# Hybrid attention and mLSTM block: mLSTM values copied into the mLSTM's load tiles, and the feed-forward shift, scale and gate sums paused over part of the second superblock

## The chip, the cores and the metric

The kernel runs on one core of a Trainium2 chip. The metric is the device time of one execution in microseconds; shown are the median and the spread of three runs, and one further execution that was profiled. A core has five engines with queues of their own: TensorE (PE; PEld is its weight load), VectorE (DVE), ScalarE (ACT), GpSimd (POOL) and SyncE (SP). SP computes nothing here and issues most of the DMA transfers, in order; POOL and ACT issue some.

## The reference

One decoder block over a sequence of 2048 rows of width 1024, in float32:

```
mod = c @ w_ada + b_ada
shift_m, scale_m, gate_m, shift_f, scale_f, gate_f = split(mod, 6)
h = rms_norm(x, g_pre_mix) * (1 + scale_m) + shift_m
q_a, k_a, v_a, q_m, k_m, v_m, o_m, i_m, f_m, g_a, g_m = split(h @ w_in)
y_a = sliding_window_attention(rope(q_a), rope(k_a), v_a, sinks)
q_m, k_m = split(silu(causal_conv4(q_m, k_m)))
y_m = sigmoid(o_m) * head_layer_norm(mlstm(q_m, k_m, v_m, i_m, f_m))
merged = sigmoid(g_a) * (y_a @ w_branch_attn) + sigmoid(g_m) * (y_m @ w_branch_mlstm)
x = x + gate_m * rms_norm(merged @ w_out, g_post_mix)
h2 = rms_norm(x, g_pre_ffn) * (1 + scale_f) + shift_f
x = x + gate_f * rms_norm((silu(h2 @ w_ffn_gate) * (h2 @ w_ffn_up)) @ w_ffn_down, g_post_ffn)
```

Attention has 8 query heads and 2 key heads of 64 with a window of 128 rows; the mLSTM has 4 heads of 128. The feed-forward width is 2816. Of `mod`, the last three parts are the feed-forward's; nothing before the feed-forward reads them.

## The kernel before, in words

The sequence is cut into four blocks of 512 rows, two to a superblock; the text calls them block one to block four (`b` 0 to 3 in the code). Every matrix product is made of three products of rounded parts (`mm3`). The mixer of a superblock runs in this order: attention queries, keys and values ("kv") and the mLSTM values (`vm`) of its first block; kv, queries and mLSTM values of its second block; then fourteen products for both blocks at once (the output gate "om", the mLSTM queries and keys "qk", the branch gates "ga" and "gm"); then the branch outputs of either block. In the first superblock the attention queries and keys of block one come in a start that is written out by hand. The feed-forward follows.

The main products go to four PSUM banks called acc, all others to four called mix. The products of the four groups of 128 rows of a block take one acc bank each, so the next stage can begin only when the copies out of PSUM have freed them. For the mLSTM values that copy is on ACT, line 870, into a tile from the pool tx, from where SP writes it to DRAM (`vm_d`); the mLSTM reads it back chunk by chunk.

The pool tx has nine tiles of 128x512 and serves nearly everything in the mixer: rotated queries and keys until POOL has written them to DRAM (`at_d`), convolutions, gates, rows of x, and the loads of the ada sums. The pool ld has four tiles of the same size. It holds the keys and values of block one, and the mLSTM's chunks of queries and keys; between the two it is free. The pool tm has nine tiles.

The `mod` sums are made on DVE: `ada_stream` loads eight pieces of `w_ada` for each half of a part (line 476, 256 KB each, on SP), and adds each, times its piece of c, into an accumulator in tm (lines 465 and 467). It is one of several Python generators that run beside the main stream of products: each says after how many ns of an estimated PE time it wants its next turn, and `tick` gives the turns between products. The stream for the feed-forward's three parts starts in the branch outputs of block one with a gap of 9000 and must be through by the branch outputs of block four (`finish(R_ada)`).

Beside it run `hprep`, which makes the normalised rows of the second block, `hsums`, which splits sums of both blocks for the fourteen products (DMA line 569, casts line 575), the attention (`attention`: tile of inputs loaded at line 954, scores copied at line 985, masked at line 987) and the mLSTM.

After the hand-written start the instructions' order on each engine is set by a scheduler from priorities and a timeline of its own; it also gives out the pools' tiles. So a change of a tile's pool or of a generator's turns can move other instructions.

Of the kernel before, what the change touches and what calls it, by code (L numbers as in the profile page):

```python
# [19 lines left out]
P = 128  # L20
# [53 lines left out]
def decoder_block(ctx: ExitStack, tc: tile.TileContext, a: dict, out: bass.AP, dbg=None):  # L74
# [386 lines left out]
    def ada_terms(acc, raw, k0, kn):  # L461
        for k in range(kn):
# [3 lines left out]
            else:  # L466
                V.scalar_tensor_tensor(acc, raw[:, k, :], c_, acc, op0=ALU.mult, op1=ALU.add)

    def ada_stream(parts, gap):
        for part, kind in parts:  # L470
            for ch in range(2):
                c0 = part * D + ch * 512
                acc = tm([P, 512])
                for k in range(KD):
                    raw = tx([P, 1, 512])
                    nc.sync.dma_start(raw, w_ada[:, c0:c0 + 512].rearrange("(p k) c -> p k c", k=KD)[:, k:k + 1, :])
                    yield gap
                    ada_terms(acc, raw, k, 1)
                if kind == "gate":
                    br = tx([1, 512])  # L480
                    nc.sync.dma_start(br, a["b_ada"][:, c0:c0 + 512])
                    yield gap
                    V.tensor_tensor(acc[0:1, :], acc[0:1, :], br, op=ALU.add)
                ada_tail(acc, part, ch, kind)
                yield gap
# [283 lines left out]
    def superblock(sb):  # L769
# [96 lines left out]

        def vm(b):
            def evac(t, ps):
                v = tx([P, 512])
                A.copy(v, ps)  # L870
                nc.sync.dma_start(vm_d[b][:, t, :], v)
            if b > 1:
                yield from token_group(kept_weights("vm"), KD, 512, lhs_h(b), evac, kept=True)
            else:
                yield from token_group(srcs_rows(w_in, KD, C_VM), KD, 512, lhs_h(b), evac, store="vm" if b else None)
# [406 lines left out]
        def outputs(b):  # L1282
# [41 lines left out]
            def before_out():  # L1324
                if b == 0:
                    finish(R["ada_m"])
                    R_ada.append(spawn(ada_stream([(4, "scale"), (3, "shift"), (5, "gate")], 9000.0)))
                if b == b1 and b + 1 < NBLK:
                    HC.clear()
                    hps[b + 1] = spawn(hprep(b + 1))  # L1330
                    rope_tables(sb + 1)
                R["gg"] = big([2, D])[:, 0, :]
                nc.sync.dma_start(R["gg"], gg_m_d)
                if b == b0:
                    end_attention(2 * NT)
                    load_y(b1, 0)
                    load_g(b1, 0)
# [15 lines left out]
        if sb == 0:  # L1353
            raws, rotated = {}, {}

            def late_q(t):
                yield from q_stream(b0, t, rope(raws[t], HQ, b0, t))

            def q_raw(t, ps):
                raws[t] = tx([P, 512])  # L1360
                A.copy(raws[t], ps)
                if t > 1:
                    R["qk"].append(spawn(late_q(t), L_KV0 + L_LATE * (t - 1)))

            def q_rope(t):
                rotated[t] = rope(raws[t], HQ, b0, t)

            def q_rest(t):
                for _ in q_stream(b0, t, rotated[t]):
                    pass  # L1370

            first.update(kv=kv0, evac=q_raw, rope=q_rope, rest=q_rest)
        else:
            yield start
            yield from q0
            yield from kv0
            yield lambda: attend(b0)
        yield from vm(b0)
# [8 lines left out]
        yield from vm1[:len(vm1) // 4]  # L1387
        yield lambda: attend(b1)
        yield from vm1[len(vm1) // 4:]

        def start_f():
            finish([hps["t"]])
# [30 lines left out]
    R_ada = []  # L1423
# [831 lines left out]
```

## Time and profile before

| | us |
|---|---|
| median of three runs | 2659.16 (2657.73 to 2660.38) |
| the profiled execution | 2668.66 |
| its span, first to last instruction | 2667.0 |
| PE busy in the span | 2615.5 (98%) |
| DVE busy | 1937.2 (73%) |
| ACT busy | 1281.9 (48%) |
| mean granted clock of PE | 0.994 |

A busy PE is one that has a product under way; it may run at half clock, which the granted clock tells. Everything that the change touches lies between 60 and about 1200 us of the span; the feed-forward begins near 1380 us.

### The profile page before, as it was taken

The numbers are of one execution on the slowest core, as the hardware profiler recorded it, in microseconds if no ns is written. First come the engines' busy times: TensorE is split into PE (matmuls) and PEld (weight loads), VectorE is DVE, ScalarE is ACT, GpSimd is POOL, SyncE is SP. The second block draws the span as 40 slices with busy tenths as digits, with TensorE's granted clock in tenths as the row PEclk, the third lists the DMA queues.
The fourth block names the chain that finished last, engine by engine and source line by source line (L and its number), as shares of the span: only waits on it lengthen the run. The fifth ranks groups of instructions, "written<-read, shape, count | busy, mean of one in ns | idle before, by whom it ended". The sixth has DMA issues, their size and how long they took to land.

```text
span 2667.0 us, 36229 instructions
## 1 busy us (share of the span) xinstructions
PE 2615.5 (98%) x12546; PEld 2145.8 (80%) x12546; DVE 1937.2 (73%) x3758; ACT 1281.9 (48%) x2531; POOL 300.3 (11%) x473
## 2 busy tenths in 40 slices
PE   8999999999989999999999999999999999999998
PEld 6877788888876788888878888888778888888876
DVE  5878887768676988875777777775776767676466
ACT  6656544545654654454643433345554333333444
POOL 0320001101132000210001111110000011001000
PEclk9899999999999999999999999999999999999999
DMA  7785465887787545597765554446675323234556
GB/s 270 255 303 164 135 196 183 291 301 253 262 313 244 166 135 181 183 296 268 220 238 193 184 169 153 163 139 228 213 242 173 111 99 116 90 111 139 199 196 220
DMA packets 327032, 532.97 MB, mean 200 GB/s; under 512 B 23136, under 2 KB 197724, under 8 KB 320064
## 3 DMA queue, kind: packets, MB, share of 16 engines
q1 hardware_dynamic: 287752, 448.45, 50.4%
q0 software_dynamic: 20880, 66.41, 6.6%
q10 hardware_dynamic: 18216, 15.79, 1.9%
q8 instruction: 99, 1.62, 0.2%
q14 instruction: 85, 0.70, 0.1%
HBM read 367.61 MB, written 154.57 MB: 196 GB/s over the span
## 4 chain that ended last, share of the span: by engine, by line
PE 88%; DVE 4%; DMA 3%; ACT 2%; issue 1%; POOL 0%; ACTq 0%; SPq 0%; DVEq 0%; POOLq 0%
PE acc L212 62%; PE mix L212 22%; PE mix L217 2%; PE acc L90 1%; DVE hl L1745 1%; PE mix L90 1%; DMA raw<-as_d 1%; ACT hl L1744 1%; DMA big<-big 0%; DMA raw<-ws_d 0%; DMA raw<-in_w_in_dram 0%; ACT tm L1002 0%; DMA at_d<-tx 0%; DMA raw<-in_w_ffn_down_dram 0%; ACT big L575 0%
## 5 line engine op out<-in xcount | busy, mean ns | idle before, releaser
L212 PE MATMUL acc<-big,hl 128*128 128x512 f32 x3936 | 936.4, 393 | 7.0 <-ACT tx L870 5.4
L212 PEld LDWEIGHTS acc<-big,hl 128*128 128x128 f32 x3936 | 733.8, 188 | 166.4 <-ACT tx L870 5.9
L1744 ACT CAST hl<-raw 128x512 fp32r<-128x512 f32 x732 | 439.9, 621 | 489.6 <-PE acc L212 208.7
L1745 DVE TENSOR_TENSOR hl<-raw,hl 128x512 fp32r<-128x512 f32 x732 | 495.1, 692 | 198.4 <-ACT hl L1744 196.0
L212 PE MATMUL acc<-whi,big 128*128 128x512 f32 (+1 forms) x896 | 281.6, 390 | 3.0 <-ACT tx L870 3.0
L212 PE MATMUL mix<-big,hl 128*128 128x512 f32 x1056 | 263.0, 390 | 1.8 <-ACT hl L1744 1.1
L212 PE MATMUL acc<-hl,hl 128*128 128x512 f32 x1008 | 237.2, 393 | 6.2 <-DVE hl L1745 3.3
L212 PEld LDWEIGHTS mix<-big,hl 128*128 128x128 f32 x1056 | 197.8, 188 | 44.5 <-ACT hl L1744 2.0
L212 PEld LDWEIGHTS acc<-hl,hl 128*128 128x128 f32 x1008 | 187.1, 188 | 51.8 <-DVE hl L1745 8.8
L212 PEld LDWEIGHTS acc<-whi,big 128*128 128x128 f32 x896 | 168.6, 192 | 36.2 <-ACT tx L870 3.4
L212 PE MATMUL mix<-hl,hl 128*128 128x512 f32 x792 | 182.7, 391 | 3.4 <-ACT hl L1744 2.6
L212 PEld LDWEIGHTS mix<-hl,hl 128*128 128x128 f32 x792 | 147.8, 188 | 37.6 <-ACT hl L1744 4.2
L212 PE MATMUL acc<-wlo,big 128*128 128x512 f32 (+1 forms) x448 | 174.4, 389 | 0.0
L212 PE MATMUL acc<-big,whi 128*128 128x512 f32 x512 | 157.3, 393 | 0.0
L268 DVE TENSOR_TENSOR wlo<-raw,whi 128x1024 fp32r<-128x1024 f32 (+1 forms) x76 | 90.8, 1194 | 65.7 <-ACT whi L267 60.2
L267 ACT CAST whi<-raw 128x1024 fp32r<-128x1024 f32 (+1 forms) x76 | 78.4, 1032 | 109.7 <-PE acc L212 103.5
L492 POOL TENSOR_TENSOR rs<-ms,halves 128x1 f32<-128x1 f32 (+1 forms) x56 | 41.3, 744 | 797.8 <-DVE ms L490 750.4
L212 PE MATMUL mix<-hcT4h,hl 128*128 128x512 f32 x352 | 115.6, 389 | 0.7 <-ACT hl L1744 0.7
L212 PE MATMUL acc<-hcT2h,hl 128*128 128x512 f32 x352 | 115.5, 389 | 0.0
L212 PEld LDWEIGHTS acc<-big,whi 128*128 128x128 f32 x512 | 95.3, 188 | 19.3
L212 PEld LDWEIGHTS acc<-wlo,big 128*128 128x128 f32 x448 | 85.8, 192 | 18.0 <-issue 1.2
L212 PE MATMUL acc<-big,wlo 128*128 128x512 f32 x256 | 97.6, 392 | 0.0
(388 smaller groups left out, 3802.3 us busy)
## 6 DMA issues: line engine op xcount, KB each, us to landing
as_d<-w POOLq DMA_DIRECT2D x154, 256.0 KB, 2.5
raw<-in_w_in_dram SPq DMA_DIRECT2D x36, 1024.0 KB, 5.4
raw<-as_d SPq DMA_DIRECT2D x70, 512.0 KB, 3.8
raw<-in_w_ffn_gate_dram SPq DMA_DIRECT2D x22, 1024.0 KB, 6.1
raw<-in_w_ffn_up_dram SPq DMA_DIRECT2D x22, 1024.0 KB, 5.8
raw<-ws_d SPq DMA_DIRECT2D x40, 512.0 KB, 4.6
tx<-in_w_ada_dram SPq DMA_DIRECT2D x64, 256.0 KB, 5.3
g_d<-tx SPq DMA_DIRECT2D x64, 256.0 KB, 2.4
```

The costliest lines, as they stand in the source:

```text
L90: self.last = tc.keep_in_program_order(f(*p, **k)).ins
L212: T.matmul(o, lhsT=lhsT, rhs=rhs, start=start, stop=stop, skip_group_check=resumed)
L217: T.transpose(o, i, ident[:k, :k])
L267: A.copy(hv, src)
L268: V.tensor_tensor(lv, src, hv.bitcast(F32), op=ALU.subtract)
L492: G.tensor_tensor(r[:, :n], ms[:, :n], nhalf[:, :n], op=ALU.pow)
L1744: A.copy(v(hi), src)
L1745: V.tensor_tensor(v(lo), src, v(hi).bitcast(F32), op=ALU.subtract)
```

## The change

Three edits. The mLSTM values of all four blocks are copied into ld tiles instead of tx tiles. A flag pauses `ada_stream` before its next load: it is set ahead of block three's keys and values and cleared after block four's mLSTM values. The stream's gap is 8000 instead of 9000.

```diff
+    held = [False]
+
+    def hold(on):
+        held[0] = on
+
     def ada_stream(parts, gap):
...
                 for k in range(KD):
+                    while held[0]:
+                        yield 1000.0
                     raw = tx([P, 1, 512])
...
             def evac(t, ps):
-                v = tx([P, 512])
+                v = ld([1, 512])[:, 0, :]
                 A.copy(v, ps)
                 nc.sync.dma_start(vm_d[b][:, t, :], v)
...
-                    R_ada.append(spawn(ada_stream([(4, "scale"), (3, "shift"), (5, "gate")], 9000.0)))
+                    R_ada.append(spawn(ada_stream([(4, "scale"), (3, "shift"), (5, "gate")], 8000.0)))
...
             yield from q0
+            yield lambda: hold(True)
             yield from kv0
...
         yield from vm1[len(vm1) // 4:]
+        yield lambda: hold(False)
```

Line numbers above 466 are seven to nine higher in the changed kernel (870 becomes 877, 476 becomes 483). The same instructions are issued in both kernels, but the order differs on every engine from block one's mLSTM values to the end of the mixer; the feed-forward's order is the same from about its first products on. Three places:

ACT in block one, from the first value copy to the attention's scores; acc are the banks of the mLSTM values, `big` the split sums. Before:

```order
L870 COPY tx_1104<-acc_938 128x512
L870 COPY tx_1113<-acc_939 128x512
L267 CAST whi_1134<-raw_935 128x528
L829 CAST tx_912<-mix_989 128x128
L803 ACTIVATE tx_945<-mix_1015 128x512
L803 ACTIVATE tx_950<-mix_1024 128x512
L575 CAST big_1495<-big_1149 128x512 x4
L870 COPY tx_1122<-acc_940 128x512
L870 COPY tx_1131<-acc_941 128x512
L985 COPY tm_1279<-mix_1281 128x256
```

Now:

```order
L877 COPY ld_1104<-acc_938 128x512
L877 COPY ld_1113<-acc_939 128x512
L877 COPY ld_1122<-acc_940 128x512
L267 CAST whi_1134<-raw_935 128x528
L836 CAST tx_912<-mix_989 128x128
L810 ACTIVATE tx_945<-mix_1015 128x512
L810 ACTIVATE tx_950<-mix_1024 128x512
L582 CAST big_1495<-big_1149 128x512 x4
L877 COPY ld_1131<-acc_941 128x512
L992 COPY tm_1279<-mix_1281 128x256
```

The third copy has moved ahead of the weight cast, the rotated keys and queries and the four casts; the fourth still stands behind them. On PE the first half of block two's key products for the third group of rows has moved with it, ahead of the first scores.

SP before block four's keys: `raw<-w_kv_d` is the load of half of the key weights, `big<-big` the copies of the split sums, `at<-at_d` an attention tile. Before:

```order
L476 DMA tx_7553<-in_w_ada_dram 128x512
L476 DMA tx_7713<-in_w_ada_dram 128x512
L569 DMA big_8010<-big_6927 128x2048
L954 DMA at_7481<-at_d_198 128x1792
L569 DMA big_8012<-big_6529 128x2048
L333 DMA raw_7547<-w_kv_d 128x2112
L476 DMA tx_7798<-in_w_ada_dram 128x512
L328 DMA whi_8117<-w_q_d 128x1024
L328 DMA wlo_8118<-w_q_d 128x1024
L333 DMA raw_7721<-w_kv_d 128x2112
```

Now:

```order
L576 DMA big_7999<-big_6930 128x2048
L576 DMA big_8001<-big_6529 128x2048
L333 DMA raw_7548<-w_kv_d 128x2112
L328 DMA whi_8103<-w_q_d 128x1024
L328 DMA wlo_8104<-w_q_d 128x1024
L961 DMA at_7482<-at_d_198 128x1792
L333 DMA raw_7716<-w_kv_d 128x2112
L878 DMA vm_d_212<-ld_7880 128x512
```

The ada loads are gone from here, and the attention tile stands behind the first key load and a query load. On PE half of block four's key products now stand ahead of the first 24 score products instead of behind them. From block three's value weights to the first load of "om", SP has nine ada loads before and none now; DVE has eight ada sums (line 465 or 467) from block three's gate scan to the softmax of its second score tile, and none now.

SP at the first load of the "om" weights (`in_w_in_dram`), at the end of block four's mLSTM values. Before:

```order
L476 DMA tx_8463<-in_w_ada_dram 128x512
L954 DMA at_8488<-at_d_202 128x1792
L1908 DMA raw_8480<-in_w_in_dram 128x8x256
L569 DMA big_8857<-big_6528 128x2048
L954 DMA at_8490<-at_d_203 128x1792
L569 DMA big_8859<-big_6926 128x2048
L1908 DMA raw_8557<-in_w_in_dram 128x8x256
L476 DMA tx_8662<-in_w_ada_dram 128x512
```

Now:

```order
L878 DMA vm_d_213<-ld_8720 128x512
L878 DMA vm_d_213<-ld_8790 128x512
L1917 DMA raw_8447<-in_w_in_dram 128x8x256
L576 DMA big_8818<-big_6528 128x2048
L576 DMA big_8820<-big_6929 128x2048
L1917 DMA raw_8524<-in_w_in_dram 128x8x256
L483 DMA tx_8825<-in_w_ada_dram 128x512
L961 DMA at_8455<-at_d_202 128x1792
```

Both weight loads now stand ahead of the attention tiles and the ada load, and two of the four value writes stand ahead of them. On PE the first 64 "om" products now follow block four's values directly; before, 12 score products stood between. The last ada load has moved from the gates "gm" to just ahead of the mLSTM's last load of values (`vmt<-vm_d`).

## Rows read from the trace of the kernel before

**Rows 1.** The page's part 1, busy time and share of the span.

```profile
PE 2615.5 (98%) x12546; PEld 2145.8 (80%) x12546; DVE 1937.2 (73%) x3758; ACT 1281.9 (48%) x2531; POOL 300.3 (11%) x473
```

**Rows 2.** Waits of PE, 60 to 880 us: total us, times, longest.

```profile
PE acc L212 <- ACT tx L870: 8.4, 4, 4.6
```

**Rows 3.** Timeline of PE: start, length, operation, count [idle before, releaser].

```profile
108.97 0.59 PE L212 MATMUL acc<-whi,big 128*128 128x264 f32 x1 [2.69 <-ACT tx L870]
...
766.18 6.15 PE L212 MATMUL acc<-raw,big 128*128 128x264 f32 x36 [4.18 <-ACT tm L985]
...
774.34 6.13 PE L212 MATMUL acc<-raw,big 128*128 128x264 f32 x48
...
784.73 1.06 PE L217 MATMUL mix<-ident,tm 128*128 128x128 f32 x8 [2.64 <-DVE tm L987]
...
800.75 0.65 PE L212 MATMUL mix<-tm,at 128*64 128x256 f32 x4 [1.26 <-ACT tm L1014]
...
858.72 7.34 PE L212 MATMUL acc<-big,hl 128*128 128x512 f32 x24 [4.55 <-ACT tx L870]
865.99 1.69 PE L212 MATMUL mix<-at 64*128 64x256 f32 x24
...
872.55 17.16 PE L212 MATMUL acc<-big,hl 128*128 128x512 f32 x74
```

**Rows 4.** Timeline of ACT.

```profile
108.34 0.59 ACT L870 COPY tx<-acc 128x512 f32<-128x512 f32 x1 [3.58 <-issue]
...
857.05 1.14 ACT L1744 CAST hl<-raw 128x512 fp32r<-128x512 f32 x2 [8.55 <-DMA raw<-in_w_in_dram]
858.09 1.07 ACT L870 COPY tx<-acc 128x512 f32<-128x512 f32 x2
```

**Rows 5.** Windows: length, busy PE, PEld, DVE, ACT, POOL, granted clock, DMA share, GB/s.

```profile
118.00:121.00 3.00, 3.00 (x16) 3.00 (x14) 0.60 (x3) 2.99 (x13) 0.00 (x0) 0.50 1.04 360
121.00:124.00 3.00, 3.00 (x20) 2.45 (x20) 1.65 (x13) 2.10 (x9) 1.75 (x2) 0.92 0.14 54
...
769.00:770.00 1.00, 1.00 (x7) 1.00 (x6) 1.00 (x4) 0.17 (x1) 0.00 (x0) 0.50 0.95 331
```

**Rows 6.** Timeline of SP, which issues DMA.

```profile
752.22 1.46 SPq L333 DMA_DIRECT2D raw<-w_kv_d  x1
...
845.62 0.40 SPq L1908 DMA_DIRECT2D raw<-in_w_in_dram  x1
...
851.95 9.66 SPq L476 DMA_DIRECT2D tx<-in_w_ada_dram  x2
...
1157.41 0.37 SPq L1084 DMA_DIRECT2D vmt<-vm_d  x1
```

**Rows 7.** DMA, 740 to 775 us; of an issue KB and us to landing.

```profile
DMA packets 2965, 11.42 MB, mean 326 GB/s; under 512 B 498, under 2 KB 498, under 8 KB 2448
...
raw<-w_kv_d SPq DMA_DIRECT2D x2, 1056.0 KB, 14.9
```

**Rows 8.** Timeline of DVE.

```profile
781.54 0.74 DVE L467 SCALAR_TENSOR_TENSOR tm<-tx,c_sb,tm 128x512 f32<-128x512 f32 x1
...
784.15 0.77 DVE L987 COPY_PREDICATED tm<-m_prev,mix 128x256 f32<-128x256 uint32 x2
...
798.04 0.75 DVE L467 SCALAR_TENSOR_TENSOR tm<-tx,c_sb,tm 128x512 f32<-128x512 f32 x1 [3.83 <-DMA tx<-in_w_ada_dram]
798.71 0.68 DVE L1035 TENSOR_TENSOR tm<-mix,tm 128x512 fp32r<-128x512 f32 x1
```

**Rows 9.** Windows after the pause, columns as in rows 5.

```profile
1030.00:1060.00 30.00, 30.00 (x146) 25.10 (x145) 27.73 (x51) 13.14 (x25) 1.66 (x1) 1.00 0.66 213
...
1150.00:1180.00 30.00, 30.00 (x164) 25.44 (x163) 19.51 (x61) 14.44 (x24) 4.11 (x4) 1.00 1.00 319
```

**Rows 10.** Lines 476 and 467: duration ns min/median/max, first and last start.

```profile
L476 SPq DMA_DIRECT2D tx<-in_w_ada_dram x64: 327/429/9170, 294.5 to 1071.1; - x64
...
L467 DVE SCALAR_TENSOR_TENSOR tm<-tx,c_sb,tm x56: 721/744/1543, 300.8 to 1078.2; 128x512 f32<-128x512 f32 x56
```

## Prediction

> **What bounds the kernel now.** I read the engine shares first: TensorE (PE) is busy for 98% of the span [rows 1], so the kernel can become faster only where PE stands still or runs slowly, not by taking work off another engine. The next view is the list of what PE waited for between 60 and 880 us, the stretch that holds everything the change touches before the sums resume. Its largest entry is the copies of the mLSTM values out of PSUM (line 870), 8.4 us in four waits [rows 2]; all its entries together are 18.8 us. The PE timeline shows the places: 2.69 us in block one, 4.18 us before block four's keys, 2.64 and 1.26 us in the attention beside them, 4.55 us before the first product of the output gate, "om" [rows 3]. Between 302 and 766 us and between 859 and 1381 us the timeline has no wait of 0.2 us or more.
>
> A wait costs more than its length here. After the 2.69 us wait the granted clock is 0.50 (1.2 GHz) until about 121.5 us: it is still 0.50 in 118 to 121 and 0.92 in 121 to 124 [rows 5]. It is also 0.50 in 769 to 770, after the 4.18 us wait [rows 5]. Products after it show the price: 36 key products took 6.15 us, 0.171 us each, where 48 took 6.13 us, 0.128 us each, a little later [rows 3]. That is 36 x 0.043 = 1.55 us lost. After the 4.55 us wait 24 products took 7.34 us, 0.306 each, against 74 in 17.16, 0.232 each [rows 3]: 1.8 us lost. After the 2.64 and 1.26 us waits the products run at their usual pace.
>
> **What the waits really end on.** The profile puts a wait down to what came last, so I read the other engines at each place.
> - Block one: ScalarE (ACT) is idle for 3.58 us before the last value copy at 108.34 [rows 4]. PE needs that copy because block two's key products use the same four PSUM banks. What the copy lacks is a tx tile, which is held by slow writes of attention keys to DRAM.
> - Block four to "om": ACT is idle for 8.55 us, and not for a tile: it waits for the gate's weights, issued at 845.62 [rows 6], casts them at 857.05, and only then comes to the copies at 858.09 [rows 4]. The tile alone is not what is late there.
> - Block four's keys: their weights were issued at 752.22 [rows 6] and such a load needs 14.9 us to land in a stretch where DMA moves 326 GB/s [rows 7]. PE goes on at 766.18, as they land.
> - Attention at 784.73: PE waits for VectorE's masked copies (line 987), which start at 784.15 behind two ada sums of 0.74 us, the first at 781.54 [rows 8].
> - Attention at 800.75: VectorE stood 3.83 us at 798.04 for the data of an ada sum; the attention output (line 1035) is behind it at 798.71 [rows 8], and PE's wait follows from that.
>
> **The change, term by term.** Gains are positive. Each has the value I take and its two ends.
>
> Term 1, block one's copies. The first three find an ld tile whose key and value writes were issued early; the fourth waits for the write of the first copy's values. It stands behind the same four casts that the third stood behind before, so it can run about where the third did, well ahead of 108.34. The 2.69 us go, and of the half-clock time (12.5 us from 108.97 to 121.5) what was PE's own: at the 41% that the row at 766.18 shows (1.55 us lost in the 3.8 us until 770) this is 5.1 us. ScalarE is full in a part of it (2.99 of 3 us in 118 to 121 [rows 5]), so I take 4. Sum 6.7; ends 0 (the new tile is as late as the old) and 7.8.
>
> Term 2, the small copy waits of blocks one and two: 8.4 - 2.69 - 4.55 = 1.2 us. From block two on nothing else holds the ld tiles. I take 1.1; ends 0 and 1.2.
>
> Term 3, block four's keys. In SP's order the attention tile (1792 columns, 0.92 MB) moves from ahead of this load to behind it, and no ada load stands beside it. At 326 GB/s [rows 7] 0.92 MB is 2.8 us. Of 4.18 us about 1.4 stay, and the clock does not fall (1.5 us). But the attention tile and the second half of the key weights are later by as much, and PE uses both within 8 us: I charge 2 us. Sum 4.18 - 1.4 + 1.5 - 2 = 2.3; ends -1 and 5.7. A rule bears on this: the Trainium skill, DMA: Bandwidth & Descriptors, section on queues, rings and completion order, says that each DMA engine consumes one ring's descriptors in ring order and takes turns between rings. By it an ada load issued after the key load cannot delay it, and the pause gives nothing here; the move of the attention tile alone would count. By share of bytes instead, the ada loads that leave this stretch would be worth about 3 us. No run here shows which holds.
>
> Term 4, VectorE in the attention. The order has eight ada sums fewer between block three's gate scan and the softmax of its second score tile; two of them (1.48 us) stand just ahead of the masked copies, and one made the 3.83 us stall. I take 1.4 of 2.64 and 1.2 of 1.26: 2.6; ends 0 and 3.9.
>
> Term 5, the "om" weights. Their load moves ahead of the attention tile and of an ada load on SP. With 2.8 us less ahead of it, 4.55 shrinks to about 1.7, and the clock does not fall: 2.8 + 1.8 = 4.6, I take 4.5. PE asks for the products earlier, since 12 scores of about 0.07 us no longer precede them (24 take 1.69 us by the row between); that is why not more. Ends 1 and 6.35. Also gone is the block of SP at 851.95, 9.66 us for two ada loads that wait for tiles [rows 6], from its old place; it reappears one place later, ahead of later weights.
>
> Term 6, what the moved sums cost. Eight more sums fall after the pause, at 0.744 us [rows 10] 6 us of VectorE. It is busy for 27.73 of 30 us in 1030 to 1060 at worst, and 19.51 of 30 in 1150 to 1180 [rows 9], and PE has no wait there: cover enough, cost nothing. Without it they would cost their 6 us. The last ada load moves from 1071.1 [rows 10] to just ahead of the last value load, which ran at 1157.41 [rows 6]: before the sums are needed, so nothing is forced. The sums' accumulator holds a tm tile through the pause, but it held one before, too. New waits from the reordering are unknown; the nearest rows give one of the smallest kind that halved the clock, 2.69 + 1.55 = 4.2 us. I take that; ends 0 and 10.
>
> The sum is 6.7 + 1.1 + 2.3 + 2.6 + 4.5 - 4.2 = 13.0 us; the ends add up to about -10 and +25. It is made against the profiled execution, 2668.66 us with a span of 2667.0, which is 9.5 us above the median of 2659.16. Some of that excess may lie in these crowded stretches, so I take 12 off the median: 2647.
>
> **The rivals.**
> A. The weights stay late. In 8.55 us ACT waited for weights and not for a tile [rows 4], and at 752.22 the key load had no ada load of the last few us ahead of it, so the pause may free nothing for either load. Terms 3 and 5 are then -1 and 1; with 4, 1 and 2 for the others and 3 for new waits the gain is 4 us: 2655. For it: two of the three big waits end on DMA, and the bytes are only moved. Against: the attention tile does move behind both loads. The ring-order rule of the Trainium skill's DMA page (DMA: Bandwidth & Descriptors) points to this case for the pause, and against it for the tile.
> B. Slower. The last ada loads now fall where DMA is full (share 1.00 in 1150 to 1180 [rows 9]), and each that waits for a tx tile holds SP, as at 851.95 for 9.66 us. Two such holds ahead of the branch weights or the attention outputs are 19 us in which the next weights are not issued. PE now has its weights well ahead there; it decides from the point at which the holds exceed this lead by more than the 12 us gained. With all 19 on PE: 2659 - 12 + 19 = 2666. Against: only one load falls there.
> C. Nothing. Block one's fourth copy waits for its new tile as long as before, and elsewhere the copies never bound; gains of 3 to 4 are eaten by the 4.2 of new waits: 2659.
> D. Everything goes, and the clock holds throughout: 25 us, 2634.
>
> **How the numbers follow.** Forecast 0.58, A 0.20, B 0.08, C 0.07, D 0.07. The likeliest case alone spans 2640 to 2653. The range 2638 to 2658 takes in A and leaves out D, B and part of C, about 0.18. A change of 0.2%, 5.3 us, is about what can be told from none. Faster by more: 0.58 + 0.07 + two thirds of A = 0.78. Slower: B and a little of C, 0.09. The rest, 0.13, is the same.
>
> **What would show it.** Right: no PE wait on the value copies in blocks one and two, and a clock of 1.00 from 107 to 121 us; the wait before block four's keys under 2 us; no ada sums on VectorE in 760 to 800; the wait before "om" under 2 us. Wrong: a new PE wait of over 3 us with half clock behind it in 750 to 880, or waits in 1100 to 1220 behind SP's ada loads. If the 4.18 and 4.55 us waits stand as they were, it is A.

## The result, and the profile after

Over 22 runs of each the changed kernel takes 2669.44 us (2662.1 to 2672.93) and the kernel before 2662.04 us (2657.73 to 2665.7). The ratio of the times is 1.0026, with a 95% interval of 1.0021 to 1.0032: slower by about 7 us, where 12 us of gain were forecast. The profiled execution of the changed kernel took 2668.51 us. That of the kernel before, on which the prediction rests, took 2668.66, which is 6.6 us above that kernel's own median of 22 runs; so a second execution of it was profiled (2661.18 us, span 2659.5). It is called the second profile of before, and the comparisons below are made with it where they can be.

PE's busy time is the old one; the changed kernel loses its time elsewhere, not in a larger amount of work:

```profile
PE 2616.6 (98%) x12546; PEld 2143.3 (80%) x12546; DVE 1940.2 (73%) x3758; ACT 1280.7 (48%) x2531; POOL 302.6 (11%) x473
```

PE's timeline after. The line numbers of this part are seven to nine higher than before, as said ahead of the prediction.

```profile
113.27 0.69 PE L217 MATMUL mix<-ident,tm 68*128 68x68 f32 x4 [3.97 <-DVE tm L919]
...
759.39 6.09 PE L212 MATMUL acc<-raw,big 128*128 128x264 f32 x48 [0.78 <-DMA raw<-w_kv_d]
...
777.52 1.17 PE L217 MATMUL mix<-ident,tm 128*128 128x128 f32 x8 [1.44 <-DVE tm L994]
780.26 2.96 PE L212 MATMUL mix<-tm,at 128*64 128x256 f32 x12 [1.57 <-DVE tm L994]
...
849.04 15.67 PE L212 MATMUL acc<-big,hl 128*128 128x512 f32 x64 [1.98 <-ACT hl L1753]
...
926.54 0.98 PE L212 MATMUL mix<-at 64*128 64x256 f32 x12 [1.56 <-DMA at<-at_d]
...
1166.20 4.14 PE L212 MATMUL acc<-big,hl 128*128 128x512 f32 x10 [3.05 <-ACT tx L1242]
1177.26 3.01 PE L212 MATMUL acc<-big,hl 128*128 128x512 f32 x12 [1.80 <-ACT tx L1894]
```

Set beside [rows 3]: the 2.69 us wait of block one is gone, but a wait of 3.97 us for the mLSTM's gate-scan rows stands 4 us later; 4.18 us before block four's keys are now 0.78; 2.64 us in the attention are now 1.44 and 1.57 in two pieces; 4.55 us before "om" are now 1.98. At 1166 and 1177 us stand two waits where the kernel before had none.

To see where the time goes, waits, half clock and slow stretches of PE together, I worked out a lost time: every product counted at the median distance to the next start for its shape at full clock (the same sum for all products in all these kernels), and the sum up to a place taken from the time at which PE reaches it. The program is cut at equal amounts of product work; a column's name is the time of that place in the second profile of before. Lost us of each stretch:

```
              60-  240-  740-  900- 1000- 1140- 1190- 1380-
             240   740   900  1000  1140  1190  1380  2658
before      15.1   2.4  20.1   0.8   0.8   0.6   1.9  20.9
before, 2nd 11.5   1.9  19.7   0.8   0.8   0.6   2.0  18.1
after       12.8   3.0  13.1   4.2   0.8   8.9   2.4  17.3
ld_only     11.8   2.8  25.2   2.5   0.8   0.6   2.0  19.3
ld_early    10.8   2.8  23.0   0.8   0.8   0.7   2.0  18.7
no_pause    12.7   3.0  25.6   3.5   0.8   0.1   2.2  18.7
gap9000     10.5   2.8  18.2  10.1   0.9   0.6   3.0  18.3
no_ld       12.9   2.3  18.8   0.5   0.8  14.8   2.4  19.5
gm_dve      11.2   3.0  13.6   4.2   0.8   6.3   2.6  17.4
tanh_late   12.1   2.9  14.4   4.3   0.8   7.6   2.5  27.5
late_only   12.8   2.2  16.7   1.9   0.8   7.4   2.5  29.9
lockstep    11.3   3.0  16.1   3.8  25.9   1.4   2.0  18.5
no_ld_ls     9.5   2.5  15.5   2.1  29.0   3.1   3.5  23.3
pb8         11.4   3.0   9.9   5.7   0.8   0.5   6.7  18.5
no_ld_pb8    9.7   2.3  16.2   1.0   0.8   0.4   4.9  17.7
cu5000      11.3   4.6  15.2   3.0   0.8   0.2   2.0  18.5
pause_cu    12.6   5.6  15.2   0.9   0.8   0.2   2.0  17.3
pause_cu2   12.6   3.9  14.4   1.8   0.8   0.2   2.0  17.9
p9_4500      9.8   4.7  18.2   7.9   0.4   0.2   2.1  16.7
```

Against the second profile of before, the changed kernel gains 6.6 us in 740 to 900, where the prediction sought its gain, loses 3.4 in 900 to 1000, loses 8.3 in 1140 to 1190, and 1 to 2 in each of the first two. All eight columns together give 7 us more, as the medians do. In the columns up to 1000 the differences depend by 1 to 2 us on how the products are grouped by shape (in coarser groups the gain in 740 to 900 comes out as 7.8 and the loss in 900 to 1000 as 4.6); the loss at 1140 to 1190 does not. The one large loss, then, lies at the branch gates of block four ("gm"), some 300 us behind the pause.

What goes on there is read on three engines of the changed kernel. First SP: the last eight loads of the gate's sum, of which these are the last four (the other four start at 1080.82, 1084.42, 1099.61 and 1101.80):

```profile
1116.88 1.00 SPq L483 DMA_DIRECT2D tx<-in_w_ada_dram  x1
1125.10 0.33 SPq L483 DMA_DIRECT2D tx<-in_w_ada_dram  x1
1131.33 0.33 SPq L483 DMA_DIRECT2D tx<-in_w_ada_dram  x1
...
1164.70 0.75 SPq L483 DMA_DIRECT2D tx<-in_w_ada_dram  x1
```

Then DVE, the sums that read them; line 465 is the first of a half, and the first row here is the last sum of the half before:

```profile
1061.38 0.74 DVE L467 SCALAR_TENSOR_TENSOR tm<-tx,c_sb,tm 128x512 f32<-128x512 f32 x1
...
1174.45 0.48 DVE L465 TENSOR_SCALAR tm<-tx,c_sb 128x512 f32<-128x512 f32 x1
...
1182.80 0.74 DVE L467 SCALAR_TENSOR_TENSOR tm<-tx,c_sb,tm 128x512 f32<-128x512 f32 x1
```

No sum runs between 1061.38 and 1174.45. Seven of the nine tx tiles are loaded by 1131.33 and then only held. In the kernel before each sum follows its load: in the second profile the eight loads run from 1014.58 to 1066.18 and the sums from 1020.58 to 1073.19. Last ACT, which copies the gates out of PSUM into tx tiles (lines 1894, 1900, 1242):

```profile
1142.25 0.58 ACT L1900 COPY tx<-acc 128x512 f32<-128x512 f32 x1 [9.79 <-DMA g_d<-tx]
...
1163.77 1.91 ACT L1264 ACTIVATE big<-big 128x2048 f32<-128x2048 f32 x1
1165.58 0.56 ACT L1242 COPY tx<-acc 128x512 f32<-128x512 f32 x1
...
1174.82 1.91 ACT L1264 ACTIVATE big<-big 128x2048 f32<-128x2048 f32 x1 [1.02 <-DMA big<-g_d]
1176.64 0.57 ACT L1894 COPY tx<-acc 128x512 f32<-128x512 f32 x1
```

A copy at 1142.25 has waited 9.79 us until a tile was free again: it had to be written to DRAM first. Both copies for which PE waits stand directly behind an activation of 1.91 us. So either the tiles or the activations, or the DMA traffic beside both, could be the cause; the experiments took these apart.

### The profile page after: what moved, and what is told of

Read it like the earlier page. It is cut to its first block, busy times and chain, and to the rows that moved or that the text cites. A ratio compares the mean times of both kernels' runs of the same rounds, so it can differ in the third digit from the quotient of the medians.

```text
span 2666.8 us, 36223 instructions
## 1 busy us (share of the span) xinstructions
PE 2616.6 (98%) x12546; PEld 2143.3 (80%) x12546; DVE 1940.2 (73%) x3758; ACT 1280.7 (48%) x2531; POOL 302.6 (11%) x473
## 4 chain that ended last, share of the span: by engine, by line
PE 89%; DVE 5%; DMA 4%; ACT 1%; issue 1%; SPq 0%; POOL 0%; ACTq 0%; DVEq 0%; POOLq 0%
PE acc L212 62%; PE mix L212 23%; PE mix L217 2%; PE acc L90 1%; DVE hl L1754 1%; PE mix L90 1%; ACT hl L1753 1%; DMA raw<-w_kv_d 1%; DMA at<-at_d 0%; DMA raw<-in_w_ffn_down_dram 0%; DMA raw<-ws_d 0%; DMA raw<-as_d 0%; DMA big<-g_d 0%; DMA big<-big 0%; DVE w L2064 0%
```

## The experiments

### The parts of the change alone

A ratio in this section is to 18 to 27 runs of the kernel before, made on the same chip as the experiment's own 4 to 12. Four kernels undo one or two parts each; the pieces of the edits are shown together. `ld_only` has the copies into ld tiles alone; `no_ld` the pause and the gap of 8000; `no_pause` the copies and the gap; `gap9000` the copies and the pause.

```diff
-                v = ld([1, 512])[:, 0, :]
+                v = tx([P, 512])
...
-            yield lambda: hold(True)
...
-                    R_ada.append(spawn(ada_stream([(4, "scale"), (3, "shift"), (5, "gate")], 8000.0)))
+                    R_ada.append(spawn(ada_stream([(4, "scale"), (3, "shift"), (5, "gate")], 9000.0)))
```

> Only the value copies go to ld tiles; no pause, gap 9000. Theory (ACT's order at the branch gates costs the time): ACT has the copies of the last gate products ahead of the branch gates' activations, as before the change, so there is no loss at 1160 to 1180 us; block one keeps its 1.8 us, so about 2660 us where before has 2662, within 0.2%. Rival 1 (late ada loads hold tx tiles and fill DMA at 1100 to 1160): the last ada load lies where it lay before, so also about 2660. Rival 2 (the ld copies themselves cost the time, by the wait for the gate scan in block one): about 2669.

> The change without its first part: copies into tx tiles, pause and gap 8000 kept. Theory: ACT has the same order at the branch gates as in the changed kernel, so waits of about 3.0 and 1.8 us come at 1160 to 1180 us, and the time is 2669 to 2671 us. Rival 1: the same, 2669 to 2671. Rival 2: about 2662 or less.

> The change without its pause: ld copies and gap 8000. Theory: the stream ends before 1071 us and ACT's order at the branch gates is that of before, so no wait over 0.3 us at 1140 to 1200 us; the waits of 2 to 5 us at 760 to 860 us come back; about 2660 us. Rival 1: about 2660 too. Rival 2: about 2669.

> The change with the old gap of 9000: ld copies and pause. The last ada loads fall still later than in the changed kernel, among the last loads of mLSTM values and behind them, but ACT has the copies ahead of most of the branch gates' activations, as before the change. Theory: the pause keeps its 4 to 6 us at 760 to 900 us and nothing is lost at 1160 to 1180 us: 2654 to 2658 us. Rival 1: the loads and their tiles are in the way more than in the changed kernel: 2669 us or more, with PE waits of over 1.5 us at 1140 to 1200 us.

> The kernel before, profiled once more, to see how much its waits differ between executions. No theory is at stake: about 2662 us. If the profile on which the prediction rests overstated the waits at 760 to 870 us, they are some 2 to 5 us shorter here.

Measured: `ld_only` 2666.10 us, ratio 1.0014 (1.0005 to 1.0023); `no_ld` 2675.70, 1.0044 (1.0030 to 1.0058); `no_pause` 2671.10, 1.0029 (1.0018 to 1.0040); `gap9000` 2672.57, 1.0032 (1.0019 to 1.0045). No part alone is faster than before. The table shows three separate costs.

The loss at 1140 to 1190 needs the pause and the gap of 8000 together: 8.9 and 14.8 with both, under 1 with one. In `no_ld` the same two copies are late, by more:

```profile
1168.65 1.66 PE L212 MATMUL acc<-big,hl 128*128 128x512 f32 x6 [3.05 <-ACT tx L1242]
...
1183.25 5.15 PE L212 MATMUL acc<-big,hl 128*128 128x512 f32 x12 [6.91 <-ACT tx L1894]
```

With a gap of 9000 the last half's loads are spread from 1109.50 to 1210.21, and only four are out by 1149.17; PE loses nothing there. But an earlier half is loaded ahead of its sums: seven pieces between 711.91 and 893.21, the first sum at 918.37. PE then waits for a gate's copy, and 10.1 us go in 900 to 1000. From `gap9000`, the first sum on DVE, then the wait on PE:

```profile
918.37 0.48 DVE L465 TENSOR_SCALAR tm<-tx,c_sb 128x512 f32<-128x512 f32 x1
```

```profile
924.54 5.92 PE L212 MATMUL acc<-big,hl 128*128 128x512 f32 x13 [5.93 <-ACT tx L1894]
```

The copies into ld tiles without the pause cost at 740 to 900: 25.2 and 25.6 against 19.7 (of this 3.3 us come in `ld_early`, below, too, whose copies there are those of before). PE comes to the "om" products before their split weights (hl) are ready. From `ld_only`, then `no_pause`:

```profile
862.57 7.77 PE L212 MATMUL acc<-big,hl 128*128 128x512 f32 x22 [2.85 <-DVE hl L1753]
```

```profile
866.24 4.21 PE L212 MATMUL acc<-big,hl 128*128 128x512 f32 x9 [4.03 <-DVE hl L1753]
```

With the pause, in `after`, this stretch costs 13.1 (18.2 in `gap9000`). So there the pause and the copies help each other, and the change does what it says.

The second profile of before also shows how much one execution's waits say. In it PE waited 1.52 and 2.06 us in block one where the first profile has 2.69:

```profile
107.05 0.39 PE L212 MATMUL acc<-whi,big 128*128 128x264 f32 x1 [1.52 <-ACT tx L870]
111.54 0.44 PE L217 MATMUL mix<-ident,tm 68*128 68x68 f32 x4 [2.06 <-DVE tm L912]
...
761.82 6.15 PE L212 MATMUL acc<-raw,big 128*128 128x264 f32 x36 [4.28 <-ACT tm L985]
```

The granted clock was back at 1.00 by 118, where [rows 5] has 0.50 in 118 to 121 (columns as there):

```profile
118.00:121.00 3.00, 3.00 (x23) 2.82 (x24) 2.58 (x14) 2.52 (x9) 1.73 (x2) 1.00 0.52 199
```

From 760 to 870 us it has nearly the waits of the first, 4.28, 2.64, 1.01 and 4.31 against 4.18, 2.64, 1.26 and 4.55, so those were not overstated.

### Late activations or late tiles

My first theory was that the two activations of 1.91 us ahead of the copies on ACT make PE wait. `gm_dve` makes the copies of the last two "gm" products of blocks three and four on DVE instead; `tanh_late` forces the first two activations behind a copy by a bias of zeros that DVE makes out of that copy's tile; `late_only` is `tanh_late` with ld tiles in blocks three and four only.

```diff
-            A.copy(u, v)
+            (V.tensor_copy if by_dve[0] else A.copy)(u, v)
...
```

```diff
+                             bias=late[1] if (b, i) == (2, 0) else 0.0)
...
+            if late[0]:
+                late[1] = small.tile([P, 1], F32, tag="late", name=nm("late"), bufs=1)
+                V.tensor_scalar(late[1], R["U2"][:, 0:1], 0.0, None, op0=ALU.mult)
```

> The changed kernel, with the copies out of PSUM of the last two gate products of blocks three and four on DVE instead of ACT; PE's order is the same up to there. Theory (these copies stand on ACT behind two activations of 1.9 us): the waits of 3.05 and 1.80 us at 1166 and 1177 us are gone or under 0.8 us, the clock stays full there, and the time is about 8 us shorter, 2660 to 2663 us. Rival 1 (the copies lack a tx tile or DMA is full): the waits stay, on whichever engine copies, and the time is about 2669 us.

> The changed kernel, in which the first two activations of block three's branch gates read a column of zeros made from the last gate product's third copy, so that ACT cannot have them ahead of the copies of the gate products before it. The ada loads and PE's order up to there are those of the changed kernel. Theory (the loss at 1150 to 1180 us is those two activations ahead of copies and of the mLSTM's work on ACT): the waits of 3.05 and 1.80 us are under 1 us each, the loss there is 0 to 2 us instead of 9, and the time is 2660 to 2663 us. Rival 1 (the ada loads there, their tiles and their share of DMA): the loss stays near 9 us and the time is 2669 us. In between, as with the copies on DVE (6 us lost): both.

> The run before this one, with ld tiles for the values of blocks three and four alone and tx tiles for blocks one and two. If the copies into ld gain in block one what the prediction said, this is 2 to 7 us slower than the run before it; if the wait there only goes over to the gate scan, it is the same or 1 to 2 us faster: 2659 to 2662 us.

Measured: `gm_dve` 2663.74 us, ratio 1.0009 (1.0000 to 1.0018), yet 6.3 us are still lost at the place; `tanh_late` 2681.94, 1.0077 (1.0065 to 1.0090), with 7.6 lost there; `late_only` 2681.28, 1.0075 (1.0062 to 1.0087), with 7.4. PE's timeline in `gm_dve`, then in `tanh_late`:

```profile
1163.68 0.33 PE L217 MATMUL mix<-ident,tm 128*128 128x128 f32 x1 [1.10 <-ACT tm L1163]
...
1168.41 1.92 PE L212 MATMUL acc<-big,hl 128*128 128x512 f32 x4 [2.28 <-DVE tx L1898]
```

```profile
1168.99 1.20 PE L212 MATMUL acc<-big,hl 128*128 128x512 f32 x4 [1.59 <-ACT tx L1243]
...
1176.25 0.49 PE L212 MATMUL mix<-cst,tm 128*128 128x129 f32 x2 [1.99 <-POOL tm L1108]
```

Whichever engine copies, and wherever the activations stand, the wait only changes its name. That theory fell. In `tanh_late` ACT, with no activation of 1.91 us ahead of it, waits with a copy for the first sum (line 465), which starts at 1176.66 and is the first to read one of the eight pieces:

```profile
1177.17 0.58 ACT L1899 COPY tx<-acc 128x512 f32<-128x512 f32 x1 [1.81 <-DVE tm L465]
```

The 2664 us of `gm_dve` against 2669 are not explained by the 2.6 us gained at the place, and I don't claim them. What `tanh_late` and `late_only` lose in the feed-forward is told at the end.

### Held tiles or the bytes

Two theories were left: the tiles that the eight pieces hold, or the 2 MB that they add to a full DMA. `lockstep` ties each load of the last half to the sum before it, by writing a column of the accumulator into the tile first; `no_ld_ls` is the same with values in tx. `pb8` loads the eight pieces into two tiles of the pool `big`, so that they hold no tx tile, and `no_ld_pb8` does it with values in tx.

```diff
+                    if (part, ch) == (5, 1):
+                        if k == 0:
+                            V.memset(acc[:, 0:1], 0.0)
+                        V.tensor_copy(raw[:, 0, 0:1], acc[:, 0:1])
```

```diff
-                    raw = tx([P, 1, 512])
+                    if (part, ch) == (5, 1) and k < 8:
+                        if k % 4 == 0:
+                            four = big([4, 512])
+                        raw = four[:, k % 4:k % 4 + 1, :]
+                    else:
+                        raw = tx([P, 1, 512])
```

> The changed kernel, in which each load of the last half of the gate's sum waits for the sum before it (a column of the accumulator is copied into the load's tile ahead of the load). In the changed kernel eight such pieces are loaded between 1081 and 1165 us and added only from 1174 us on, so that seven of the nine tx tiles are held from 1131 us. Theory (the held tiles make the gate copies late and cost the 9 us; that ACT has activations ahead of them follows from it): at most two tiles are held, PE has no wait over 1 us at 1140 to 1200 us, and the time is 2659 to 2663 us, although the loads and their bytes now lie wholly in 1140 to 1200 us or behind it. Rival 1 (the loads' share of DMA there): 2669 us or more.

> The same with tx tiles for the values. Without lockstep this version had waits of 3.05 and 6.91 us at 1168 and 1183 us and 2675.7 us. Theory: both waits go, about 14 us, so 2660 to 2663 us; against the run before this one it shows whether the ld tiles gain anything beside the pause. Rival 1: 2675 us.

> The changed kernel, with the eight pieces of the last half of the gate's sum loaded into two tiles of the pool big instead of eight of tx. PE's order is that of the changed kernel up to the gates gm. The eight loads, 2 MB, now stand on SP all at the place of the last one, ahead of block three's last loads, so that their bytes fall at about 1145 to 1170 us, and their sums as late as before. Theory (held tx tiles): the gate copies get tiles in time, PE has no wait over 1 us at 1140 to 1200 us, and the loss there is 0 to 2 us instead of 9: 2659 to 2663 us. Rival 1 (bytes on full DMA): more bytes than in the changed kernel fall there, so 9 us or more are lost and the time is 2669 us or more.

> The same with tx tiles for the values, to which 2675.7 us belong with the pieces in tx. Theory: the waits of 3.05 and 6.91 us at 1168 and 1183 us go, so 2660 to 2663 us; the difference to the run before this one is what the ld tiles are worth beside the pause. Rival 1: 2675 us.

Measured: `lockstep` 2684.97 us, ratio 1.0090 (1.0076 to 1.0104); `no_ld_ls` 2693.19, 1.0119 (1.0103 to 1.0136). They told nothing on the question: the loss at 1140 to 1190 is down to 1.4 and 3.1, but the order moved, and 25.9 and 29.0 us are lost before it, where PE stands for the mLSTM's chain, as in this row of `lockstep`:

```profile
1115.06 0.47 PE L217 MATMUL mix<-ident,tm 128*128 128x128 f32 x1 [3.89 <-DVE tm L1101]
```

`pb8` took 2661.36 us, ratio 0.9999 (0.9990 to 1.0008), and `no_ld_pb8` 2661.78, 1.0000 (0.9991 to 1.0009): 8 us below `after`, and 14 below `no_ld`, with 8.4 and 14.4 us fewer lost at 1140 to 1190. In `pb8` the eight loads leave SP in one burst, some 10 us ahead of the place where PE waited in `after`. SP, DVE and the windows of `pb8`:

```profile
1151.69 4.02 SPq L488 DMA_DIRECT2D big<-in_w_ada_dram  x6
1156.93 0.97 SPq L488 DMA_DIRECT2D big<-in_w_ada_dram  x2
```

```profile
1165.80 0.48 DVE L465 TENSOR_SCALAR tm<-big,c_sb 128x512 f32<-128x512 f32 x1
...
1175.90 0.75 DVE L467 SCALAR_TENSOR_TENSOR tm<-big,c_sb,tm 128x512 f32<-128x512 f32 x1
```

```profile
1160.00:1170.00 10.00, 10.00 (x60) 8.68 (x59) 7.71 (x14) 5.02 (x11) 1.29 (x1) 1.00 1.04 421
```

The same window of `after`:

```profile
1160.00:1170.00 10.00, 6.95 (x30) 5.52 (x29) 4.48 (x21) 8.02 (x13) 2.85 (x3) 0.83 1.06 337
```

More bytes pass in `pb8` (421 GB/s against 337), DMA is as full in both, and PE is busy throughout at full clock where in `after` it stands for three tenths of the window and half of the rest of it is slow. So the bytes are not the cause. Three things differ: no tx tile is held, all loads but the last are some 25 to 70 us later, and ACT's order at the gates is another one. Its first activation of 1.91 us starts at 1160.35 in `after`, and at 1172.99 in `pb8`, behind copies again, as in the kernel before. The scheduler gives out the tiles and sets the order by them, so I take that order as what the held tiles do; changed alone, in `tanh_late`, it left 7.6 us of the loss. A kernel that loads early into tiles of neither pool was not tried. `pb8` loses 4.3 us more than `after` in 1190 to 1380, where PE waits 2.04 us at 1202.50 for a load into a `big` tile, and 3.2 less in 740 to 900, where PE's order is the same; that its whole gain equals the loss taken away is in part luck.

### A smaller gap after the pause; block one

If the pieces are held because the stream comes late to its end, a smaller gap after the pause should bring the last half forward, to where before has it. `cu5000` is the changed kernel with that; `pause_cu` has it with values in tx (`pause_cu2` repeats it); `p9_4500` goes from 9000 to 4500, with values in tx. `cu5000_ms` also zeroes the gate-scan rows early on POOL, for block one's new wait. `ld_early` is the kernel before with ld tiles for blocks one and two only.

```diff
-                    yield gap
+                    yield 5000.0 if resumed[0] else gap
...
```

```diff
-                v = tx([P, 512])
+                v = ld([1, 512])[:, 0, :] if b < 2 else tx([P, 512])
```

> The changed kernel, with a gap of 5000 instead of 8000 once the pause is over, so that the last ada load lies ahead of the gates gm, earlier than before the change. Theory: ACT then has the copies ahead of the branch gates' activations, nothing is lost at 1140 to 1200 us, and 760 to 900 us is as in the changed kernel: 2660 to 2663 us. Rival 3 (the pause costs its time where the sums are resumed, at 860 to 1000 us, by DVE and DMA work): more sums fall there, so waits of some us at 860 to 1000 us and 2669 us or more.

> The kernel of the run before this one, with the zeroing of the gate scan's rows issued on POOL ahead of the gate products of each block instead of within the scan. In the changed kernel DVE waits 1.05 us for this zeroing, behind POOL's writes of attention keys, before PE's 3.97 us wait in block one. If POOL is what bounds block one, the wait at 113 us falls to about 2.9 us and the time by 1 to 2 us. If DVE's own work ahead of the scan bounds it, the wait stays over 3.5 us and the time is the same.

> The pause alone, with the sums made up early: tx tiles for all value copies, gap 8000 up to the pause and 5000 after it. Theory: the pause is worth some 3 to 6 us at 750 to 900 us, and nothing is lost at 1140 to 1200 us, so 2657 to 2661 us. If the pause gains only together with the ld tiles, it is 2662 us or more.

> The pause alone with tx tiles, gap 8000 and 5000, timed once more on the chip of the run before this one: 2657 to 2660 us, 0.1 to 0.2% under the kernel before.

> The pause alone with tx tiles, gap 9000 up to it and 4500 after it. The pause with a gap of 8000 up to it lost 3.7 us at 650 to 700 us, where the old gap loses nothing, and gained the rest. Theory: that loss goes and the gain at 750 to 900 us stays, so 2654 to 2657 us. If the loss at 650 to 700 us comes from the pause and not from the gap, 2658 us.

> The kernel before, with ld tiles for the values of blocks one and two alone; no pause, gap 9000. Theory (in blocks three and four the earlier copies let PE run into split weights of om that are not ready, which cost the run with ld tiles alone its time at 850 to 870 us; in block one nothing is gained): 2661 to 2663 us, without the 2.85 us wait for the split weights. Rival (the copies in block one cost the time): 2666 us, as with ld tiles for all blocks.

Measured: `cu5000` 2664.98 us, ratio 1.0004 (0.9995 to 1.0013); `cu5000_ms` 2666.19, 1.0017 (1.0009 to 1.0026); `pause_cu` 2658.62, 0.9987 (0.9978 to 0.9996), and on the repeat 2661.20, 0.9997 (0.9986 to 1.0008); `p9_4500` 2669.69, 1.0031 (1.0019 to 1.0042); `ld_early` 2665.10, 1.0010 (1.0002 to 1.0019).

The smaller gap takes the loss at 1140 to 1190 away (0.2 us in the four that the table has), so that much of the theory holds without a change of pool. `pause_cu` is the nearest to a gain, but the repeat doesn't bear it out; no version was found that clearly beats the kernel before. `pause_cu` wins 4 to 5 us in 740 to 900, in both profiles, and loses 2 to 4 in 240 to 740. `p9_4500` was to be rid of the latter and loses 2.8 there still; it has eight pieces of one half loaded from 875.57 on, with the first sum at 945.65, and loses 7.9 in 900 to 1000, where PE waits 0.95 and 2.19 us for split weights and 1.24 us for a gate's copy. One fact limits the theory: `cu5000` too holds seven pieces for a while (loaded 881 to 939, sums from 951.23), and PE has no wait over 0.4 us there. Held tiles cost where the copies need them, not everywhere.

`ld_early` is 3 us slower than before, with 23.0 lost in 740 to 900, where only the order had moved: copies into ld tiles in block one are worth nothing that these runs can show. PE only comes sooner to the next wait, for the gate scan. In `cu5000`, then in `cu5000_ms`, which differs from it by the early zeroing alone:

```profile
112.20 0.69 PE L217 MATMUL mix<-ident,tm 68*128 68x68 f32 x4 [2.85 <-DVE tm L921]
```

```profile
111.87 0.69 PE L217 MATMUL mix<-ident,tm 68*128 68x68 f32 x4 [2.86 <-DVE tm L921]
```

So in these two the zeroing on POOL doesn't bind; DVE, which waits for nothing there, is still at work ahead of and in the scan. The wait is 2.84 to 2.97 in `ld_only`, `ld_early`, `gap9000`, `gm_dve` and `pb8` too. In the profiled execution of the changed kernel POOL adds about 1 us to it:

```profile
108.36 0.72 POOL L840 DMA_DIRECT2D at_d<-tx  x1 [5.49 <-issue]
109.08 1.64 POOL L813 DMA_DIRECT2D at_d<-tx  x3
110.71 0.54 POOL L914 MEMSET tm<- 68x512 f32 x1
```

```profile
111.28 0.68 DVE L917 TENSOR_TENSOR tm<-tm,tm 4x512 f32<-4x512 f32 x1 [1.05 <-POOL tm L914]
```

POOL stands until 108.36, and an earlier write of attention keys, issued at 99.66, takes 8.4 us to land; in the first profile of before such a write (9.5 us from 98.73) lands just ahead of the late copy of [rows 4]. POOL's zeroing follows, and DVE's gate scan waits 1.05 us for that. The clock falls in this execution as in the first profile of before, 4 us later:

```profile
118.00:121.00 3.00, 3.00 (x15) 3.00 (x15) 0.45 (x3) 2.99 (x15) 0.00 (x0) 0.50 1.00 300
```

## Why the prediction was wrong

**Two steps failed, term 6 and, as large, term 1.** Between the 13.0 us forecast and the 7 us lost lie 20 us; by the table some 7.5 of them are term 6, 9.1 terms 1 and 2 together, 2.8 terms 3 to 5, and 1.1 the stretch 240 to 740, to which the prediction gave nothing.

**Term 6** failed in two sentences: "cover enough, cost nothing", and that the last ada load moves to "before the sums are needed, so nothing is forced". I priced the moved sums as DVE time and the moved loads as a place on SP, and I looked at tm, where the accumulator is held, but not at the tx tiles in which loaded pieces wait for their sums. Taken at -4.2 us with ends of 0 and -10, the term measured about -12: 8.3 at 1140 to 1190 by held tiles (shown by `pb8`, `no_ld_pb8` and the kernels with a smaller gap), and 3.4 in 900 to 1000, a new wait from the reordering, which the term was to cover as well. Of the latter the row at 926.54 shows 1.56 us, a wait for an attention tile. The table puts it with ld tiles in the second superblock (`ld_only` 2.5, `no_pause` 3.5, against 0.8 of `ld_early` and 0.5 of `no_ld`), though not without exception: `no_ld_ls` and `pause_cu2`, with tx tiles, have 2.1 and 1.8. What carries it from the one to the other stays open.

**Term 1** (block one, +6.7): the value copy is early, as said, and gains nothing. The stretch 60 to 240 lost 12.8 us against 11.5; over the table it is 11.6 in the mean of the ten kernels with ld tiles in block one and 11.8 in the nine rows with tx tiles. I removed the wait that ended last and did not ask what ends next: DVE's gate scan, for which PE waited 2.06 us in the second profile of before already, and now waits 2.24 to 3.97. The size was also taken from one execution in which the stretch was at its worst (15.1 against 11.5 in the second).

**Term 2** (+1.1): right in that the waits on the copies of blocks one and two are gone; what they were worth can't be told apart from term 1.

**Term 3** (block four's keys, +2.3): right in place and near in size: 4.18 went to 0.78 where 1.4 was expected. The cause is the attention tile that moved behind the load, not the ada loads that left, and the DMA issues show it. Of the first key load, columns as in [rows 7], in `no_pause`, with one ada load close ahead of it on SP (746.76), two behind it (749.90 and 752.60), and the attention tile behind too:

```profile
raw<-w_kv_d SPq DMA_DIRECT2D x1, 1056.0 KB, 11.4
```

The second profile of before, with the attention tile ahead and one ada load behind:

```profile
raw<-w_kv_d SPq DMA_DIRECT2D x1, 1056.0 KB, 14.0
```

In `ld_early`, with the same loads around it, it is 15.1, and in `ld_only`, with the attention tile ahead and two ada loads behind, 15.3. In the changed kernel, with no ada load beside it, PE goes on 11.6 us after its issue at 747.79. So ada loads beside it did not delay it by an amount that shows; with the attention tile ahead it took 2.6 to 3.9 us more, about what was reckoned for that tile. The Trainium skill (DMA: Bandwidth & Descriptors, section on queues, rings and completion order) says that each DMA engine takes a ring's descriptors in ring order, though a later one may finish its write before an earlier one. These rows agree with the order, and what the prediction gave for the case without that rule, 3 us for the ada loads, has no support.

**Term 4** (attention, +2.6): the ada sums are gone from there, but the scheduler put the rotation of block four's keys in their place, ahead of the masked copies (line 994). DVE after:

```profile
774.73 1.61 DVE L798 TENSOR_TENSOR tx<-tx,cos 128x128 f32<-128x128 f32 x1
776.27 0.28 DVE L797 TENSOR_TENSOR tx<-tx,sin 128x128 f32<-128x128 f32 x1
776.94 0.43 DVE L994 COPY_PREDICATED tm<-m_prev,mix 128x256 f32<-128x256 uint32 x1
```

The two waits of 2.64 and 1.26 became 1.44 and 1.57: 0.9 us gained.

**Term 5** ("om", +4.5): the wait is 1.98 in the changed kernel, near the 1.7 expected. But the runs that keep this order have 3.28 (`gm_dve`), 4.52 (`tanh_late`), 4.12 (`lockstep`) and 0.74 (`pb8`): a mean of 2.9 of the five, against 4.55 and 4.31 in the two profiles of before. The wait shrinks by about 1.5 where 2.85 was expected, and a single execution can't show it.

Terms 3 to 5 together are the 6.6 us of 740 to 900 (of `gm_dve`, `tanh_late`, `lockstep`, `pb8` and `after` the mean is 6.3), where 9.4 were expected. The gain sought by the change is there, and it is lost again behind it.

**The rivals.** B had the side, the place (1150 to 1180) and nearly the time, 2666, but by SP standing still for 19 us; SP's last ada load held it for 0.75 us, and ACT's copies waited for tiles instead. A was right for the ada loads, wrong for the attention tile. C had block one right. D never came near. What the prediction named as a sign of being wrong, "waits in 1100 to 1220 behind SP's ada loads", is where the loss was found. The range ended at 2658 because B was held to be one case in twelve on the ground that "only one load falls there": in fact the whole last half's sums did, and the order of the changed kernel could have told that.

**The base.** The working was made against a profiled execution that was 6.6 us above its kernel's median. "Some of that excess may lie in these crowded stretches" was right: 3.6 of the lost time in 60 to 240 was not there in the second profile. Taking 12 of 13 off the median was too little of a discount.

## What to carry to other kernels

When loads are moved in time, count for every pool how many tiles are loaded and not yet read at each place, not only the time of the instructions that read them: eight prefetched pieces whose sums came 18 to 94 us after their loads took up a pool of nine, and copies out of PSUM far from the change were late. Where a wait is to be removed, ask what PE waits for next (behind the late copy stood the gate scan) before it is counted as a gain. And take a gain of a few us from more than one profiled execution.

## What the runs showed that was not expected

Where PE's order is the same, its waits differ between executions by 2 us and more (0.74 to 4.52 before "om" in five kernels), and the clock makes more of it: around the waits in block one the granted clock was 0.50 for 13.7 us in the first profile of before (107.8 to 121.5) and for 3.4 us in the second (113.6 to 117.1).

`tanh_late` and `late_only` lose 9 and 12 us more than the second profile of before in the feed-forward (27.5 and 29.9 against 18.1; the other rows have 16.7 to 23.3), though they change no code there. They have one tile of one column more, in the pool `small`, which should move the tiles that lie behind it. Groups of instructions from 1500 to 2400 us, with busy time and mean ns of one, in `tanh_late` and in the second profile of before:

```profile
L212 PE MATMUL mix<-hcT4h,hl 128*128 128x512 f32 x280 | 93.7, 396 | 0.0
```

```profile
L212 PE MATMUL mix<-hcT4h,hl 128*128 128x512 f32 x280 | 91.9, 389 | 0.0
```

The same products take 396 ns in place of 389. All four groups that read hcT are slower by 6 to 7 ns, 840 products in this stretch, which makes about 5.5 us. That the tiles' place in memory is the cause was only argued; no run moved them alone.
